# Renewing the sample states in the FFN instead of in the head groups' stage

## The chip, the cores and the metric

One Trainium2 chip; the kernel runs on one of its cores. The metric is the time in microseconds (us) that one execution takes on the device, the median of several runs. The engines are TensorE (PE in the profile; its weight loads are PEld), VectorE (DVE), ScalarE (ACT), GpSimd (POOL) and SyncE (SP), which here only issues loads.

## The reference

One step of a hybrid decoder layer, on 256 tokens of a prompt and on 8 samples of 8 tokens each, in float32. The part that matters here is the state of the SSD heads (a recurrence over tokens). Per sample b there are 32 heads with a state of 64 x 128 each. In the reference it is, in short:

```python
states = einsum("bcsgn,bcsgr,bcsgrp->bcgrpn", bc, decay_states, xdt)   # B^T (decay * dt * x)
final  = chunk_decay * init_state + states                             # the state after the 8 tokens
y_off  = einsum("bctgn,bcgrpn,bctgr->bctgrp", cc, states_in, exp(da_cs))   # C times the old state
...
y = y_diag + y_off + d_skip * x
```

For the samples the old state is an input (`state_ssm`, 8 x 32 x 64 x 128, 8.4 MB) and the new one an output of the same size. Two things are done with an old state: C times it goes into y, and so into everything that follows; and it is renewed, that is, scaled by the decay over the eight tokens, and grown by a product of B and of x times its step and decay. The renewed state is only an output: nothing in the layer reads it.

After the heads come an output projection, a norm, and an FFN: a projection up to 11264 columns, a convolution over three tokens, a gate, and a projection down.

## The kernel before

All 320 tokens (256 + 64) are the moving operand of every weight matmul. Each weight matrix is read once, in slabs of 128 x 1024 numbers (`slab`, L110 to L124): SP loads a slab into one of three buffers, ACT rounds it to `whi` (L117), DVE subtracts to make `wlo` (L119), and TensorE multiplies three times per block of 128 x 128 (`accumulate`, L126 to L130: whi by the high part of x, whi by the low part, wlo by the high part), 24 matmuls per slab. `project` (L152) makes 512 columns of a projection up, and `chunk_out` (L199) the share that 512 rows have in a projection down.

The stages in order: the input projection with the gated MLP (gate), which `chunk_out` adds to the output; then, from L686, the head groups' stage, four groups of eight heads (`ssd(g)`, L713), with the projections of z and of the next group's x between them; the last chunks of the output projection; a norm (L993 to L1034); the FFN (L1038 on), in eleven groups of 512 columns: `ffn_up(g+1)` and then `chunk_out(ffn_w_down, g)`; the last norm.

Side work is written as generators that stand in the list `bg`. `tick` (L140) moves the first of them on by one step; `project` and `chunk_out` call it after their slabs, `rate` times (1 or 2). `finish` runs a task to its end. This fixes the order in which instructions are traced. A planner then orders each engine's queue by priority and by its own cost model: slabs have a high priority, evacuations of PSUM under `first()` a higher one, side work none. On the chip each queue runs in that order; an instruction that waits holds all behind it on its engine, and an SP load that waits for a buffer holds the loads behind it.

The states, four pairs i per group, each of two tiles `st` of 128 x 512 (samples i and 4 + i):

- `load_state(i)` (L719) loads a pair on SP, into five buffers. Two pairs are loaded when the group begins, the others when a pair has been worked off (L846).
- `with_c(i, st)` (L793, matmuls L798, out `yo_ps`) multiplies by C: eight small matmuls, traced a step after a yield.
- `picked(i)` (L801) makes `bm` on ACT: B's rows of this pair of samples, out of `bsp` by the column mask `bsel`.
- `shrunk(i, st)` (L806) scales both tiles on POOL by `tote` (exp of the sum of the decays, made in `steps`, L498).
- `grown(st, bm)` (L811) multiplies `bm` by `xsp` into a bank `up_ps` (L814), and DVE adds it to the tile (L815).
- `store_state` (L818) writes the tile out, issued from ACT's queue.
- `xsp` is `xq` split into a high and a low part: a copy on ACT (L778) and a subtraction of the upper 64 rows on DVE (L779).

Groups 0 to 2 do all of it in `ssd`. Group 3 only applies C there; its states are loaded a second time and renewed by `renewals` (L822) while the last two chunks of the output projection run (L979, L985), and its last pair of matmuls stands behind the last chunk (L995), ahead of the sums of the norm.

PSUM has eight banks: four for weight matmuls (tag "mm"), four (tag "ms", `misc`) for everything else, `yo_ps` and `up_ps` among them.

Of the kernel before, what the change touches and what calls it, by code (L numbers as in the profile page):

```python
# [9 lines left out]
F32 = mybir.dt.float32  # L10
# [7 lines left out]
P = 128  # L18
# [16 lines left out]
def hybrid_step(  # L35
# [267 lines left out]
    dacs_d = dr.tile([NH, NT + NS], F32, name="dacs_d")  # L303
    tot_d = dr.tile([NH, NB], F32, name="tot_d")


# [45 lines left out]
    def by_token(ps, x, c):  # L352

        pe.transpose(ps, x[:, P * c:P * c + P], ident)

    def fourfold(out, x):
# [5 lines left out]
    with ExitStack() as mctx:  # L362
# [43 lines left out]
        ed = op.tile([P, 4, 4], F32, name="ed")  # L406
        tote = op.tile([P, NH, NB], F32, name="tote")

        def steps():
# [276 lines left out]
        with tc.tile_pool(name="sd", bufs=1) as sd:  # L686
# [8 lines left out]
            for c in range(4):  # L695
# [11 lines left out]
            def by_head(ap):  # L707
                return ap.rearrange("p (h d) -> p h d", d=64)

# [3 lines left out]
            def ssd(g):  # L713
# [18 lines left out]

                sts = [load_state(i) for i in range(2)]

# [41 lines left out]
                x0d = decayed(0, 0)  # L776
                xsp = sd.tile([P, 2, 512], F32R, tag="xsp", name="xsp", bufs=1)
                act.copy(xsp, xq)  # L778
                dve.tensor_tensor(out=xsp[64:], in0=xq[64:], in1=xsp[64:].bitcast(F32), op=ALU.subtract)  # L779
# [20 lines left out]

                def picked(i):  # L801
                    bm = sd.tile([P, 2, P], F32R, tag="bm", name="bm", bufs=2)
                    act.activation(bm, bsp[:, :, bs].bitcast(F32), AF.Copy, scale=bsel[:, i:i + 1])
                    return bm

                def shrunk(i, st):  # L806
                    for h in range(2):
                        pool.tensor_tensor(out=by_head(st[h]), in0=by_head(st[h]),  # L808
                                           in1=tote[:, h0:h0 + 8, 4 * h + i:4 * h + i + 1].to_broadcast([P, 8, 64]), op=ALU.mult)

                def grown(st, bm):  # L811
                    for h in range(2):
                        ps = misc("up_ps")
                        made = pe.matmul(ps, bm[:, h], xsp[:, h], start=True, stop=True)  # L814
                        dve.tensor_tensor(out=st[h], in0=st[h], in1=ps, op=ALU.add)  # L815
                    return made.ins

                def store_state(i, st, by=act):  # L818
                    for h in range(2):
                        by.dma_start(o_ssm_s[4 * h + i, g], st[h])  # L820

                def renewals():  # L822
                    sts = [load_state(i) for i in range(2)]
                    yield
                    for i in range(4):
                        st, bm = sts.pop(0), picked(i)
                        shrunk(i, st)
                        yield
                        made = grown(st, bm)
                        store_state(i, st, act if i < 3 else pool)  # L830
                        if i < 2:
                            sts.append(load_state(2 + i))
                        yield made

                for i in range(4):
# [5 lines left out]
                    yield  # L841
                    if g < 3:
                        shrunk(i, st)
                        grown(st, bm)
                        store_state(i, st)
                    if i < 2:  # L846
                        sts.append(load_state(2 + i))

# [144 lines left out]
            with first():  # L993
                with tc.issue_after(pd_last[-1]):
                    made = next(rest[0])  # L995
                with tc.issue_after(made):
                    most = token_sums(sq2)
                with tc.issue_after(sums_ins[-1]):
                    ps = token_sums(*one)
                with tc.issue_after(sums_ins[-1]):  # L1000
                    made = next(rest[1])
                r = rsqrt_by_root(most, ps, 1.0 / D)
                behind = rsqrt_ins[-1]
                with tc.issue_after(behind):
                    next(rest[1])
                with tc.issue_after(made):
                    r2b = spread(r)
# [30 lines left out]
    with tc.tile_pool(name="fp", bufs=1) as fp:  # L1038
# [226 lines left out]
```

## Time and profile before

| | us |
|---|---|
| median of three runs | 1821.66 |
| lowest and highest | 1821.31, 1822.76 |
| the profiled execution's span | 1821.3 |
| the input projection and the gate, about | 0 to 440 |
| the head groups' stage, about | 440 to 760 |
| the last chunks of the output projection, about | 760 to 855 |
| norm and beginning of the FFN, about | 855 to 905 |
| the FFN, about | 905 to 1800 |
| last norm and output | 1800 to 1821 |

The profiled execution's own time is its span, 1821.3 us, which agrees with the fastest of the three runs; nothing beside the span is counted.

How to read the profile: a line such as `L814 PE MATMUL up_ps<-xsp,bm` is line 814 of the kernel, on TensorE, writing the tile `up_ps` from `xsp` and `bm`. A row of waits, `PE yo_ps L798 <- DMA st: 3.1, 3, 1.2`, says that this line waited for that producer for 3.1 us in total, three times, 1.2 at the longest. A matmul's bar is longer than its share of the time, since matmuls overlap: the distance from start to start is what it costs. The granted clock is a share of TensorE's full clock.

### The profile page before, as it was taken

What the parts mean: (1) busy time and instruction counts of PE and PEld (TensorE: products, weight loads), DVE (VectorE), ACT (ScalarE), POOL (GpSimd) and SP (SyncE); (2) the same over time, 40 slices, a digit from 0 to 9 for tenths busy, and PEclk for the clock granted to TensorE, in tenths of its full rate; (3) what the DMA queues carried; (4) which work ended last, traced back from release to release, by engine and by line L of the source; (5) the groups of instructions that cost most, each with busy time, mean ns of one, the idle gap of its engine ahead of it and who ended that gap; (6) DMA issues with size and microseconds to landing.
All of it is one profiled execution on the core that took longest, in us unless ns stands there. A gap on an engine that the chain in (4) does not pass through costs nothing.

```text
span 1821.3 us, 31186 instructions
## 1 busy us (share of the span) xinstructions
PE 1789.4 (98%) x12222; PEld 1751.6 (96%) x12222; DVE 1182.3 (65%) x2029; ACT 798.1 (44%) x1102; POOL 304.5 (17%) x626
## 2 busy tenths in 40 slices
PE   8999999999999999999899999999999999999998
PEld 8999999999889899999899999999999999999997
DVE  5449664557977868677776465647465665756575
ACT  6444454334535445444455433333334343433334
POOL 3102200000331312104521010101111010101004
PEclk9999999999999999999999999999999999999999
DMA  8656544455566565556454545444545445454542
GB/s 268 186 150 189 159 132 152 155 157 176 189 192 189 162 196 173 156 159 206 148 149 151 150 153 153 151 152 151 153 152 154 150 154 150 151 148 153 151 154 99
DMA packets 222947, 294.66 MB, mean 162 GB/s; under 512 B 16752, under 2 KB 150736, under 8 KB 222608
## 3 DMA queue, kind: packets, MB, share of 16 engines
q1 hardware_dynamic: 210544, 270.21, 48.6%
q10 hardware_dynamic: 9872, 14.82, 2.2%
q0 software_dynamic: 2384, 7.64, 1.4%
q8 instruction: 96, 1.57, 0.4%
q14 instruction: 51, 0.42, 0.1%
HBM read 277.80 MB, written 14.82 MB: 161 GB/s over the span
## 4 chain that ended last, share of the span: by engine, by line
PE 88%; DVE 4%; DMA 2%; issue 2%; POOL 2%; ACT 1%; ACTq 0%; POOLq 0%; DVEq 0%
PE ps L128 18%; PE ps L130 18%; PE ps L129 18%; PE pd L128 9%; PE pd L130 9%; PE pd L129 9%; DVE wlo L119 1%; PE y_ps L888 1%; DMA cT<-in_x_tok 1%; POOL acc_mix L1023 1%; ACT whi L117 1%; DMA cs<-dacs_d 1%; DMA st<-in_state_ssm 0%; POOL st L808 0%; PE sg L650 0%
## 5 line engine op out<-in xcount | busy, mean ns | idle before, releaser
L119 DVE TENSOR_TENSOR wlo<-wraw,whi 128x1024 fp32r<-128x1024 f32 (+1 forms) x476 | 592.0, 1244 | 455.4 <-ACT whi L117 452.8
L117 ACT CAST whi<-wraw 128x1024 fp32r<-128x1024 f32 (+1 forms) x476 | 496.3, 1043 | 730.2 <-PE ps L129 443.7
L128 PE MATMUL ps<-h_hi,whi 128*128 128x320 f32 x2528 | 787.5, 312 | 8.6 <-ACT whi L117 5.6
L130 PE MATMUL ps<-h_hi,wlo 128*128 128x320 f32 x2528 | 783.9, 310 | 4.3 <-DVE wlo L119 4.3
L129 PE MATMUL ps<-h_lo,whi 128*128 128x320 f32 x2528 | 782.8, 310 | 0.0
L128 PEld LDWEIGHTS ps<-h_hi,whi 128*128 128x128 f32 x2528 | 477.5, 189 | 14.2 <-ACT whi L117 6.9
L130 PEld LDWEIGHTS ps<-h_hi,wlo 128*128 128x128 f32 x2528 | 477.2, 189 | 6.6 <-DVE wlo L119 6.4
L129 PEld LDWEIGHTS ps<-h_lo,whi 128*128 128x128 f32 x2528 | 477.5, 189 | 0.7 <-issue 0.5
L128 PE MATMUL pd<-fhi,whi 128*128 128x320 f32 x704 | 217.0, 308 | 0.0
L129 PE MATMUL pd<-flo,whi 128*128 128x320 f32 x704 | 217.0, 308 | 0.0
L130 PE MATMUL pd<-fhi,wlo 128*128 128x320 f32 x704 | 217.0, 308 | 0.0
L128 PE MATMUL pd<-ohi,whi 128*128 128x320 f32 x448 | 140.8, 314 | 0.0
L129 PE MATMUL pd<-olo,whi 128*128 128x320 f32 x448 | 139.5, 311 | 0.0
L130 PE MATMUL pd<-ohi,wlo 128*128 128x320 f32 x448 | 139.4, 311 | 0.0
L128 PEld LDWEIGHTS pd<-fhi,whi 128*128 128x128 f32 x704 | 132.1, 188 | 0.0
L129 PEld LDWEIGHTS pd<-flo,whi 128*128 128x128 f32 x704 | 132.1, 188 | 0.0
L130 PEld LDWEIGHTS pd<-fhi,wlo 128*128 128x128 f32 x704 | 132.1, 188 | 0.0
L1074 POOL COPY ptf<-pad 128x2 f32<-128x2 f32 x88 | 20.5, 233 | 618.1 <-DVE pad L1062 617.4
L211 DVE TENSOR_TENSOR acc_ffn<-acc_ffn,pd 128x320 f32<-128x320 f32 x160 | 77.5, 484 | 38.7 <-PE pd L130 37.4
L128 PEld LDWEIGHTS pd<-ohi,whi 128*128 128x128 f32 x448 | 84.8, 189 | 2.9 <-issue 1.6
L130 PEld LDWEIGHTS pd<-ohi,wlo 128*128 128x128 f32 x448 | 84.7, 189 | 1.0 <-issue 1.0
L129 PEld LDWEIGHTS pd<-olo,whi 128*128 128x128 f32 x448 | 84.8, 189 | 0.5 <-issue 0.2
(297 smaller groups left out, 1599.4 us busy)
## 6 DMA issues: line engine op xcount, KB each, us to landing
wraw<-in_ffn_w_up SPq DMA_DIRECT2D x176, 512.0 KB, 3.7
wraw<-in_w_in SPq DMA_DIRECT2D x144, 512.0 KB, 3.7
wraw<-in_ffn_w_down SPq DMA_DIRECT2D x88, 512.0 KB, 3.5
wraw<-in_w_out SPq DMA_DIRECT2D x64, 512.0 KB, 3.5
st<-in_state_ssm SPq DMA_DIRECT2D x40, 256.0 KB, 3.8
out_ssm_state_sample<-st ACTq DMA_DIRECT2D x30, 256.0 KB, 3.6
cs<-dacs_d SPq DMA_DIRECT2D x16, 320.0 KB, 4.3
xr<-in_xT SPq DMA_DIRECT2D x4, 640.0 KB, 4.8
```

What stands on the lines that cost most here:

```text
L117: act.copy(hi[:, :m], raw[:, :m])
L119: dve.tensor_tensor(out=lo[:, :m], in0=raw[:, :m], in1=hi[:, :m].bitcast(F32), op=ALU.subtract)
L128: pe.matmul(ps, whi, xhi, start=first, stop=False)
L129: pe.matmul(ps, whi, xlo, start=False, stop=False)
L130: return pe.matmul(ps, wlo, xhi, start=False, stop=last).ins
L211: dve.tensor_tensor(out=acc[:, nb, :], in0=acc[:, nb, :], in1=ps[:, :NT], op=ALU.add)
L888: pe.matmul(ps[64 * i:64 * i + 64, cols], w(hl), x(hl, m, cpx), tile_position=(0, 64 * i), **flags)
L1023: added.append((dve if kt < 2 else pool).tensor_tensor(out=a, in0=a, in1=xr[q][:, k, :], op=ALU.add).ins)
L1074: pool.tensor_copy(ptf[:, k, :], pad[:, 256:258])
```

## The change

In the head groups' stage only C is applied to the states, for all four groups. All sixteen pairs are loaded a second time in the FFN and renewed there, by a task in `bg` that begins with `ffn_up(1)` and is finished at the latest ahead of the last chunk. Its operands are kept in DRAM until then: `xq` of each group (512 KB each), `bsp` (512 KB) and `tote` (128 KB) are stored from ACT's queue, and loaded again from SP's. The split of `xq` into `xsp` moves to the FFN too, in two halves. In the head groups' stage the state tiles get eight buffers, so that a group's four pairs are there together. In the FFN they get four, and the operands lie in two tiles that the output projection no longer needs.

```diff
+    xq_d = dr.tile([4, P, 2, 512], F32, name="xq_d")
+    bsp_d = dr.tile([P, 2, 512], F32, name="bsp_d")
+    tote_d = dr.tile([P, NH, NB], F32, name="tote_d")
...
+            tote = op.tile([P, NH, NB], F32, name="tote")
             sp.dma_start(tote, tot_d.unsqueeze(0).broadcast_to([P, NH, NB]))
             act.activation(tote, tote, AF.Exp)
+            yield
+            act.dma_start(tote_d, tote)
...
+            act.dma_start(bsp_d, bsp.bitcast(F32))
...
-                    st = [sd.tile([P, 512], F32, tag="st", name="st", bufs=5) for _ in range(2)]
+                    st = [sd.tile([P, 512], F32, tag="st", name="st", bufs=8) for _ in range(2)]
...
-                sts = [load_state(i) for i in range(2)]
+                sts = [load_state(0), load_state(1)]
...
+                sts.append(load_state(2))
                 yield
+                act.dma_start(xq_d[g], xq)
...
-                xsp = sd.tile([P, 2, 512], F32R, tag="xsp", name="xsp", bufs=1)
-                act.copy(xsp, xq)
-                dve.tensor_tensor(out=xsp[64:], in0=xq[64:], in1=xsp[64:].bitcast(F32), op=ALU.subtract)
...
+                sts.append(load_state(3))
                 yield
...
-                def picked(i):
...
-                def shrunk(i, st):
...
-                def grown(st, bm):
...
-                def store_state(i, st, by=act):
...
-                def renewals():
...
-                for i in range(4):
-                    if g < 3:
-                        bm = picked(i)
+                for i in range(4):
                     yield
-                    st = sts.pop(0)
-                    with_c(i, st)
+                    with_c(i, sts[i])
                     yield
-                    if g < 3:
-                        shrunk(i, st)
-                        grown(st, bm)
-                        store_state(i, st)
-                    if i < 2:
-                        sts.append(load_state(2 + i))
...
-                    rest.extend([renewals(), final()])
-                    next(rest[0])
+                    rest.append(final())
...
-            bg.append(chain(repeat(None, 1), islice(rest[0], 4)))
             chunk_out(w_out, 6, *res[2], False, rate=2)
...
-            bg.append(islice(rest[0], 3))
...
                 with tc.issue_after(pd_last[-1]):
-                    made = next(rest[0])
-                with tc.issue_after(made):
                     most = token_sums(sq2)
...
+        def renewals():
+
+            kept = hp.tile([P, 4, NT], F32R, tag="ohi", name="kept").rearrange("p k n -> p (k n)")
+            more = hp.tile([P, 4, NT], F32R, tag="olo", name="xsp").rearrange("p k n -> p (k n)")
+            tote = kept[:, :NH * NB].bitcast(F32).rearrange("p (h b) -> p h b", b=NB)
+            bsp = kept[:, 256:512].rearrange("p (h n) -> p h n", h=2)
+            bms = [kept[:, 512 + 256 * i:768 + 256 * i].rearrange("p (h n) -> p h n", h=2) for i in range(2)]
+            xsp = more[:, :1024].rearrange("p (h n) -> p h n", h=2)
+            sp.dma_start(tote, tote_d)
+
+            def load(g, i):
+
+                st = [fp.tile([P, 512], F32, tag="st", name="st", bufs=4) for _ in range(2)]
+                for h in range(2):
+                    sp.dma_start(st[h], state_ssm[4 * h + i, g])
+                return st
+
+            ahead = [load(0, 0)]
+            yield
+            for g in range(4):
+                h0 = 8 * g
+                sp.dma_start(bsp.bitcast(F32), bsp_d[:, :, P * g:P * g + P])
+                for h in range(2):
+                    raw = fp.tile([P, 512], F32, tag="raw", name="raw", bufs=1)
+                    sp.dma_start(raw, xq_d[g, :, h])
+                    yield
+                    yield
+                    act.copy(xsp[:, h], raw)
+                    dve.tensor_tensor(out=xsp[64:, h], in0=raw[64:], in1=xsp[64:, h].bitcast(F32), op=ALU.subtract)
+                    yield
+                for i in range(4):
+                    st = ahead.pop(0)
+                    bm = bms[i % 2]
+                    act.activation(bm, bsp.bitcast(F32), AF.Copy, scale=bsel[:, i:i + 1])
+                    for h in range(2):
+                        pool.tensor_tensor(out=by_head(st[h]), in0=by_head(st[h]),
+                                           in1=tote[:, h0:h0 + 8, 4 * h + i:4 * h + i + 1].to_broadcast([P, 8, 64]), op=ALU.mult)
+                    yield
+                    yield
+                    if (g, i) != (3, 3):
+                        ahead.append(load(g + (i + 1) // 4, (i + 1) % 4))
+                    for h in range(2):
+                        ps = misc("up_ps")
+                        pe.matmul(ps, bm[:, h], xsp[:, h], start=True, stop=True)
+                        dve.tensor_tensor(out=st[h], in0=st[h], in1=ps, op=ALU.add)
+                        yield
+                    yield
+                    for h in range(2):
+                        act.dma_start(o_ssm_s[4 * h + i, g], st[h])
+                    yield
+
         NG = NF // 4
         nxt = ffn_up(0)
+        grow = renewals()
+        bg.append(grow)
...
             if g == NG - 1:
+                finish(grow)
                 root_table(pd_last[-1])
```

More of the change, by code (lines that the diff above doesn't have):

```diff
@@ L354, in by_token, with by_head @@
         pe.transpose(ps, x[:, P * c:P * c + P], ident)
+    def by_head(ap):
+        return ap.rearrange("p (h d) -> p h d", d=64)
     def fourfold(out, x):
@@ L406, in hybrid_step @@
         ed = op.tile([P, 4, 4], F32, name="ed")
-        tote = op.tile([P, NH, NB], F32, name="tote")
         def steps():
@@ L705, in hybrid_step @@
                         dve.tensor_tensor(out=b[rs], in0=ps[rs], in1=b[rs].bitcast(F32), op=ALU.subtract)
-            def by_head(ap):
-                return ap.rearrange("p (h d) -> p h d", d=64)
+            act.dma_start(bsp_d, bsp.bitcast(F32))
             x_of = {0: x0}
@@ L799, in with_c @@
                                       start=i == 0, stop=i == 3, tile_position=(0, row))
-                def picked(i):
-                    bm = sd.tile([P, 2, P], F32R, tag="bm", name="bm", bufs=2)
-                    act.activation(bm, bsp[:, :, bs].bitcast(F32), AF.Copy, scale=bsel[:, i:i + 1])
-                    return bm
-                def shrunk(i, st):
-                    for h in range(2):
-                        pool.tensor_tensor(out=by_head(st[h]), in0=by_head(st[h]),
-                                           in1=tote[:, h0:h0 + 8, 4 * h + i:4 * h + i + 1].to_broadcast([P, 8, 64]), op=ALU.mult)
-                def grown(st, bm):
[L812 to L816, printed above, removed]
-                def store_state(i, st, by=act):
-                    for h in range(2):
-                        by.dma_start(o_ssm_s[4 * h + i, g], st[h])
-                def renewals():
-                    sts = [load_state(i) for i in range(2)]
-                    yield
-                    for i in range(4):
-                        st, bm = sts.pop(0), picked(i)
-                        shrunk(i, st)
-                        yield
-                        made = grown(st, bm)
-                        store_state(i, st, act if i < 3 else pool)
-                        if i < 2:
-                            sts.append(load_state(2 + i))
-                        yield made
-                for i in range(4):
-                    if g < 3:
-                        bm = picked(i)
-                    yield
-                    st = sts.pop(0)
-                    with_c(i, st)
-                    yield
-                    if g < 3:
-                        shrunk(i, st)
-                        grown(st, bm)
-                        store_state(i, st)
-                    if i < 2:
-                        sts.append(load_state(2 + i))
+                for i in range(4):
+                    yield
+                    with_c(i, sts[i])
+                    yield
                 for r in range(2):
@@ L1000, in hybrid_step @@
                 with tc.issue_after(sums_ins[-1]):
-                    made = next(rest[1])
+                    made = next(rest[0])
                 r = rsqrt_by_root(most, ps, 1.0 / D)
@@ L1004, in hybrid_step @@
                 with tc.issue_after(behind):
-                    next(rest[1])
+                    next(rest[0])
                 with tc.issue_after(made):
```

## The prediction

> **What bounds the kernel now.** I read the page first, then the table of busy time by stage, then TensorE's waits stage by stage, then the timeline around the longest of them.
>
> ```profile
> span 1821.3 us, 31186 instructions
> PE 1789.4 (98%) x12222; PEld 1751.6 (96%) x12222; DVE 1182.3 (65%) x2029; ACT 798.1 (44%) x1102; POOL 304.5 (17%) x626
> ```
>
> TensorE is busy for 98% of the span, so at most 32 us (1821.3 - 1789.4) of plain idle time can be won. The question is where they lie. Columns below: stretch, its length, then for each engine its busy time and instruction count, granted clock, DMA share, GB/s.
>
> ```profile
> 440.00:760.00 320.00, 311.74 (x2222) 285.63 (x2221) 254.20 (x485) 151.77 (x230) 79.61 (x99) 0.99 0.59 184
> 760.00:855.00 95.00, 94.87 (x647) 94.23 (x646) 69.04 (x123) 44.91 (x67) 17.67 (x15) 1.00 0.57 183
> 855.00:905.00 50.00, 41.70 (x256) 39.13 (x255) 42.12 (x64) 26.72 (x46) 27.74 (x34) 0.95 0.43 137
> 950.00:1400.00 450.00, 450.00 (x3071) 450.00 (x3070) 265.28 (x429) 183.72 (x232) 54.87 (x176) 1.00 0.50 152
> 1800.00:1822.00 22.00, 13.04 (x63) 8.84 (x61) 12.32 (x28) 4.96 (x9) 7.86 (x7) 0.83 0.31 120
> ```
>
> In the FFN TensorE has no gap at all: 3071 matmuls in 450 us are 146.5 ns each, so a slab of 24 takes 3.52 us. The head groups' stage (440 to 760) leaves 8.3 us idle, the hand-over to the FFN (855 to 905) 8.3 us, the tail 9.0 us. The change touches the first of these, so its gain is to be found in this stage's waits:
>
> ```profile
> PE yo_ps L798 <- DMA st<-in_state_ssm: 3.1, 3, 1.2
> PE up_ps L814 <- DVE st L815: 2.0, 1, 2.0
> PE tsum L263 <- DVE ssq L282: 1.1, 1, 1.1
> PE up_ps L814 <- DVE xsp L779: 1.1, 1, 1.1
> PE y_ps L888 <- DVE cs L877: 0.8, 1, 0.8
> ```
>
> These add up to 8.1 us, the whole of the idle time there. Three rows, 6.2 us, belong to the states: a state that has not landed (3.1), and renewing matmuls that wait for a bank or an operand (2.0 + 1.1).
>
> **The change part by part.** *The waits.* The two up_ps rows leave this stage with the matmuls that wait: -3.1 us. The yo_ps row should go too. Now five buffers serve a group, and a state is loaded only when an older one has been scaled, grown and stored; afterwards eight buffers hold the whole group, the loads are issued in its first three steps and each buffer is free as soon as C has been applied to it. A load lands in 3.8 us (row further down), and from the issue of the last pair of states to its use lie more than six steps. So -3.1 us. For each the bounds are 0, if another wait takes the place, and its full row; I take the full rows, since the DVE, which would be late next, loses work as well (below).
>
> *The clock.* After the longest wait the matmuls run slowly for a while:
>
> ```profile
> 485.60 0.50 PE L814 MATMUL up_ps<-xsp,bm 128*128 128x512 f32 x1 [1.97 <-DVE st L815]
> ...
> 486.89 0.47 PE L128 MATMUL pd<-ohi,whi 128*128 128x320 f32 x1
> ...
> 490.09 0.34 PE L128 MATMUL pd<-ohi,whi 128*128 128x320 f32 x1
> ```
>
> ```profile
> 487.00:490.30 3.30, 3.30 (x15) 3.30 (x14) 3.30 (x5) 1.31 (x4) 0.61 (x3) 0.52 0.26 80
> ```
>
> From 486.89 to 490.09 twelve matmuls take 3.20 us, 267 ns each, 120 ns over the usual 146.5: 1.5 us lost at a granted clock of 0.52. Bounds 0 and 1.5; I take 1.5, because the slow stretch begins 1.3 us after the end of the 1.97 us wait and nothing else stopped TensorE near it. The Trainium skill ("TensorE: Matmul & The Clock Gate", Part 1: The HAM clock gate) says that the clock falls to half after an idle window of about 3.4 us. By that figure a wait of 1.97 us would not have been enough, there would be no such term, and the forecast would be 1.5 us higher; the row shows the half clock after the shorter wait, so I follow the row.
>
> *The order on TensorE.* A pair of renewing matmuls between the matmuls of the weights costs less than one that follows C's matmuls:
>
> ```profile
> 536.86 0.74 PE L814 MATMUL up_ps<-xsp,bm 128*128 128x512 f32 x2
> 537.43 0.31 PE L128 MATMUL ps<-h_hi,whi 128*128 128x320 f32 x1
> ```
>
> ```profile
> 812.27 0.62 PE L814 MATMUL up_ps<-xsp,bm 128*128 128x512 f32 x2
> 812.73 0.31 PE L128 MATMUL pd<-ohi,whi 128*128 128x320 f32 x1
> ```
>
> By the starts of the next matmuls the pair took 0.57 us behind C and 0.46 us alone. Twelve pairs leave the stage and all of them then stand among weight matmuls: between 0 and 12 x 0.11 = 1.3 us; I take 1.0, since one or two of them stand alone already. Otherwise the pairs' 0.46 us only move: TensorE is full where they go. The three pairs of the last group that are moved from 760 to 855 gain nothing, as that stretch is full as well (94.87 of 95). The last pair is a small loss:
>
> ```profile
> 855.90 0.63 PE L814 MATMUL up_ps<-xsp,bm 128*128 128x512 f32 x2
> 856.37 0.72 PE L263 MATMUL tsum<-ones,sq 128*128 128x1 f32 x6
> 857.42 0.83 PE L263 MATMUL tsum<-ones,sq 128*128 128x1 f32 x6 [0.33 <-ACT sq L297]
> ```
>
> It fills time before sums that wait for ACT's square in any case; its removal saves nothing there, and it costs 0.46 us in the FFN: +0.5 (bounds 0 and 0.5).
>
> *What is added to the FFN.* Durations, min/median/max in ns, from the lines as they run now:
>
> ```profile
> L808 POOL TENSOR_TENSOR st<-st,tote x32: 1057/1065/2378, 459.7 to 831.7; 128x512 f32<-128x512 f32 x32
> L815 DVE TENSOR_TENSOR st<-st,up_ps x32: 671/680/689, 466.2 to 857.1; 128x512 f32<-128x512 f32 x32
> L803 ACT ACTIVATE bm<-bsp,bsel x16: 493/508/511, 450.8 to 817.3; 128x256 fp32r<-128x256 f32 x16
> L778 ACT CAST xsp<-xq x4: 1045/1050/1052, 455.5 to 718.8; 128x1024 fp32r<-128x1024 f32 x4
> L779 DVE TENSOR_TENSOR xsp<-xq,xsp x4: 1222/1223/2049, 458.7 to 721.5; 64x1024 fp32r<-64x1024 f32 x4
> L820 ACTq DMA_DIRECT2D out_ssm_state_sample<-st x30: 338/338/1282, 466.9 to 838.0; - x30
> ```
>
> DVE: 32 x 0.68 + 4 x 1.22 = 26.7 us. ACT: 16 x 0.51 + 4 x 1.05 = 12.3 us, and 32 x 0.34 = 10.9 us of issuing stores. POOL: 32 x 1.07 = 34 us, 76 at the longest duration. The renewals yield 121 times; the FFN ticks after each slab but those of its first and last steps, 24 times per group, so they run for 121 x 3.52 = 426 us, some five of the eleven groups, and are through well before the last chunk. Over that time DVE goes from 59% (265.28 of 450) to about 65%, ACT from 41% to about 46%. SP issues 32 state loads and 13 of operands. Traffic: 8.4 MB of states in and 8.4 out, 2.1 of xq, 0.4 of the rest, 19.3 MB in 426 us, 45 GB/s on top of 152. The head groups run at 184 GB/s with such traffic today:
>
> ```profile
> wraw<-in_w_in SPq DMA_DIRECT2D x45, 512.0 KB, 4.2
> ...
> st<-in_state_ssm SPq DMA_DIRECT2D x37, 256.0 KB, 3.8
> out_ssm_state_sample<-st ACTq DMA_DIRECT2D x24, 256.0 KB, 3.6
> ```
>
> ```profile
> wraw<-in_ffn_w_up SPq DMA_DIRECT2D x176, 512.0 KB, 3.7
> ```
>
> A weight slab lands there in 4.2 us against 3.7 in the FFN, and TensorE waited for no slab. What covers all this is the lead with which slabs are made:
>
> ```profile
> 1201.28 1.05 ACT L117 CAST whi<-wraw 128x1024 fp32r<-128x1024 f32 x1 [2.47 <-PE ps L129]
> ```
>
> ```profile
> 1202.36 1.23 DVE L119 TENSOR_TENSOR wlo<-wraw,whi 128x1024 fp32r<-128x1024 f32 x1 [2.29 <-ACT whi L117]
> ```
>
> ACT starts a slab when TensorE has released one of three buffers, so two slabs, 7.04 us, lie ahead; 2.31 us later (1203.59) the new one is ready: 4.7 us of lead. The densest stretch of the FFN is where the second half is evacuated:
>
> ```profile
> 1233.00:1255.00 22.00, 22.00 (x152) 22.00 (x151) 19.55 (x41) 10.72 (x14) 5.93 (x16) 1.00 0.47 148
> ```
>
> A pair of states takes six steps, 21 us, so such a stretch gets one pair, 1.36 us of DVE, at times half of an xsp (0.6), into 2.45 us of idle time, with the lead behind it. I put the FFN at 0. Bounds: 0, and 16 pairs at one POOL operation each that shows in full, 17 us (the third rival).
>
> *New waits in queues.* SP's state load waits until a buffer has been stored: the store is issued three steps (10.5 us) before and lands in 3.6. SP's load of the second half of xq waits for the DVE that splits the first, one step earlier; behind it stand weight loads, and 4.7 us of lead. On ACT each store waits for the DVE's add, two steps earlier, with the next cast behind it. On TensorE the renewing matmul waits for bm (0.5 us, two steps earlier). All of these I cost at 0 for the same cover. The operands' stores (four of xq, one of B, one of decays) are 6 x 0.34 us on ACT, which has over half its time free.
>
> *What DVE and POOL lose in the head groups' stage.* 24 adds and the four splits, 24 x 0.68 + 4 x 1.22 = 21 us of DVE's 254, and POOL's 24 scalings. That is why I let no new wait in: DVE is the engine that would be late next.
>
> **The sum.** -3.1 - 3.1 - 1.5 - 1.0 + 0.5 = -8.2 us on the profiled 1821.3 gives 1813.1. That execution is the fastest of the three shown; their median, 1821.66, lies 0.36 us above it, so I forecast **1813.5**.
>
> **The rivals.**
> *More goes than the states' own waits (1810.1).* With 21 us less on DVE the sums no longer wait for ssq (1.1) nor y_ps for cs (0.8), and the slow clock after the former (674.5 to 678) shrinks; without it 1813.5 - 1.9 = 1811.6, with its 1.5 us 1810.1. For it: both waits are for DVE. Against: cs also waits for its own load, ssq for a chain through ACT.
>
> ```profile
> 674.50:678.00 3.50, 3.50 (x15) 3.50 (x14) 2.46 (x10) 1.04 (x1) 0.00 (x0) 0.52 0.81 262
> 454.00:486.00 32.00, 30.03 (x206) 27.20 (x205) 30.13 (x60) 17.90 (x28) 13.73 (x23) 1.00 0.51 164
> ```
>
> *DVE keeps the pace (1819.1).* Ahead of the longest wait DVE is busy for 30.13 of 32 us. If its convolutions and sums merely stop TensorE a little later, only the loads' 3.1 us are won, less 0.5 in the FFN: 1821.66 - 2.6. For it: that stretch. Against: some 4 us of its work leave.
>
> *The FFN pays (1830.5).* DVE takes its instructions in order, and the add of a state stands in front of evacuations and splits. If POOL has not finished scaling by then, they all wait:
>
> ```profile
> DVE st L815 <- POOL st L808: 5.1, 5, 3.7
> ```
>
> The add comes two steps (7.0 us) after the scaling was issued, which itself takes 2.1 us a pair, 4.8 at the longest. If in each of 16 pairs 1.06 us shows on TensorE, that is +17.0 on the forecast: 1830.5. It is slower than before from 0.5 us per pair on. Against it: 2.2 to 4.9 us of cover and then the lead. The Trainium skill ("SBUF — State Buffer", Who interferes with whom) speaks for it: a VectorE instruction with two SBUF inputs and a GpSimd one that reads SBUF exclude each other for a whole instruction. The trace agrees: a split took 2.08 us instead of 1.23 beside two scalings. By that rule 32 x 1.06 = 34 us of holding are moved into the FFN.
>
> ```profile
> 486.36 2.08 DVE L119 TENSOR_TENSOR wlo<-wraw,whi 128x1024 fp32r<-128x1024 f32 x1
> ```
>
> **How the numbers follow.** Forecast 0.52, more goes 0.12, DVE keeps the pace 0.22, the FFN pays 0.14. The range 1809.0 to 1821.5 holds the first three and leaves out the last and a little below. What a measurement of this kernel can tell from no change is about 0.2%, 3.6 us: the first two cases are faster (0.64), the third is within it (0.22), the last slower (0.14).
>
> **What would show it.** Right: in the head groups' stage no wait of yo_ps for a state and none of up_ps, 5 to 6 us less idle time, a full clock at 487; in the FFN still no wait. Wrong: TensorE waits for wlo or up_ps between 910 and 1340, a split's lead well under 4 us, DVE's add waiting for POOL, or waits for cs and ssq grown in the head groups.

## The result, and the profile after

The changed kernel takes 1810.26 us (median of four runs, 1808.37 to 1812.42) against 1822.21 us for the kernel before, now also four runs (1821.31 to 1823.06): a ratio of 0.9936, 95% interval 0.9924 to 0.9949, so 11.7 us or 0.64% less. The forecast was 1813.5 us, 8.2 us less; the time lies within the range, and next to the figure of the first rival (1810.1).

A word on the base. The changed kernel's profiled execution took 1812.42 us at a span of 1810.7 us: an execution's time is its span and 1.7 us around it. The profiled execution of before, with its span of 1821.3, must then be the one of 1823.06 us, the slowest of the four and not the fastest, as the prediction had taken it.

The page of the kernel after, and its busy time by stage (the stages' bounds are shifted by what was won):

```profile
span 1810.7 us, 31220 instructions
PE 1784.3 (99%) x12222; PEld 1750.2 (97%) x12222; DVE 1183.4 (65%) x2033; ACT 798.7 (44%) x1106; POOL 303.2 (17%) x624
```

```profile
440.00:755.00 315.00, 314.41 (x2311) 293.19 (x2311) 238.18 (x477) 150.85 (x226) 45.06 (x70) 1.00 0.56 179
755.00:850.00 95.00, 91.72 (x605) 90.07 (x605) 67.71 (x128) 45.35 (x71) 18.95 (x17) 0.96 0.47 154
850.00:900.00 50.00, 45.48 (x287) 44.03 (x286) 37.43 (x47) 22.41 (x36) 30.04 (x31) 0.93 0.58 179
945.00:1340.00 395.00, 395.00 (x2676) 393.62 (x2675) 262.56 (x415) 167.16 (x221) 79.00 (x174) 1.00 0.60 193
1790.00:1811.00 21.00, 12.65 (x61) 8.45 (x59) 11.98 (x27) 4.96 (x9) 7.71 (x6) 0.84 0.33 125
```

In the head groups' stage TensorE idles 0.6 us instead of 8.3, at a full clock. The 3.3 us of idle time between 755 and 850 are no new waits: the hand-over to the FFN now begins there, and its longest wait, 2.1 us for `h_hi`, lay between 855 and 905 before. While the renewals run in the FFN (945 to 1340) it has no gap, though 193 GB/s move instead of 152. TensorE's waits in the head groups' stage, all of them:

```profile
PE tsum L263 <- DVE ssq L282: 0.5, 1, 0.5
```

Of the five rows of before one is left, at half its size. Where the time went is best read from three marks that both kernels have: C's matmuls (`yo_ps`), the first matmuls of the FFN's first step (`ps_one`), and the hand-over at the end (`x1p`). The rows give the first and the last start. Before:

```profile
L798 PE MATMUL yo_ps<-st,cb_cms x128: 379/391/403, 459.0 to 731.0; 128*32 128x256 f32 x128
L128 PE MATMUL ps_one<-h_hi,whi x16: 307/308/313, 914.4 to 922.7; 128*128 128x320 f32 x16
L1147 PE MATMUL x1p<-acc_mix,ident x22: 432/433/863, 1803.8 to 1815.1; 128*128 128x320 f32 x22
```

After:

```profile
L804 PE MATMUL yo_ps<-st,cb_cms x128: 378/391/404, 462.0 to 713.1; 128*32 128x256 f32 x128
L128 PE MATMUL ps_one<-h_hi,whi x16: 304/309/310, 896.6 to 904.9; 128*128 128x320 f32 x16
L1159 PE MATMUL x1p<-acc_mix,ident x22: 432/433/803, 1793.5 to 1804.7; 128*128 128x320 f32 x22
```

| stretch, us | before | after | difference |
|---|---|---|---|
| beginning to the first C matmul | 459.0 | 462.0 | +3.0 |
| first to last C matmul | 272.0 | 251.1 | -20.9 |
| last C matmul to the FFN's first step | 183.4 | 183.5 | +0.1 |
| FFN | 889.4 | 896.9 | +7.5 |
| last norm and output | 17.5 | 17.2 | -0.3 |
| span | 1821.3 | 1810.7 | -10.6 |

So the head groups' stage gave 21 us, much more than forecast (8.7 us by the four terms, and 5.6 us for 24 moved matmuls), and the FFN took 7.5 us back, the price of all 32 matmuls. The adds in the FFN and the scalings ahead of them:

```profile
L1129 DVE TENSOR_TENSOR st<-st,up_ps x32: 676/686/690, 948.0 to 1339.1; 128x512 f32<-128x512 f32 x32
```

```profile
L1120 POOL TENSOR_TENSOR st<-st,kept x32: 1057/1138/2455, 882.4 to 1303.1; 128x512 f32<-128x512 f32 x32
```

The adds spread over 391 us; from the FFN's first step (896.6) to the last add it is 443 us, against the 426 that the prediction counted from the steps. DVE never waited for POOL at an add.

### The profile page after: what moved, and what is told of

Its sections match the earlier page's. It is cut to its first block, busy times and chain, and to the rows that moved or that the text cites. A ratio compares the mean times of both kernels' runs of the same rounds, so it can differ in the third digit from the quotient of the medians.

```text
span 1810.7 us, 31220 instructions
## 1 busy us (share of the span) xinstructions
PE 1784.3 (99%) x12222; PEld 1750.2 (97%) x12222; DVE 1183.4 (65%) x2033; ACT 798.7 (44%) x1106; POOL 303.2 (17%) x624
## 4 chain that ended last, share of the span: by engine, by line
PE 93%; DVE 2%; DMA 2%; ACT 1%; POOL 1%; issue 1%; ACTq 0%; DVEq 0%; POOLq 0%
PE ps L128 19%; PE ps L130 19%; PE ps L129 19%; PE pd L128 10%; PE pd L130 10%; PE pd L129 10%; DMA wraw<-in_w_in 1%; PE y_ps L851 1%; DVE wlo L119 1%; POOL acc_mix L981 1%; PE yo_ps L804 1%; ACT whi L117 0%; PE sg L658 0%; PE up_ps L1128 0%; PE xt_ps L357 0%
## 5 line engine op out<-in xcount | busy, mean ns | idle before, releaser
L211 DVE TENSOR_TENSOR acc_ffn<-acc_ffn,pd 128x320 f32<-128x320 f32 x160 | 77.1, 483 | 35.8 <-PE pd L130 34.8
```

Of the source, the lines that this page charges most:

```text
L211: dve.tensor_tensor(out=acc[:, nb, :], in0=acc[:, nb, :], in1=ps[:, :NT], op=ALU.add)
```

## The experiments

The theory after the result: TensorE's waits in the head groups' stage came from the renewals' POOL and DVE work there and from late states, and the FFN pays for the moved matmuls alone. The rivals are named with each run. "As changed" means the time of the changed kernel, 1809.8 to 1810.3 us; a difference from it is taken from 1809.78.

**Both kernels once more, for second traces.** No edit.

> The kernel before, unchanged, for a second trace. If the first 440 us differ between the two kernels' profiles (3.0 us in the changed kernel's disfavour) only by chance, this trace will show another offset there, by 1 us or more; if the beginning is the same in every execution, it agrees within 0.5 us with the first trace up to 440 us. In the head groups' stage both views expect the same waits again: yo_ps for states near 3 us, up_ps near 3 us, y_ps and tsum near 2 us, and two stretches at half clock.

> The changed kernel, unchanged, for a second trace. Chance at the beginning: its first 440 us come out up to 3 us shorter than in the first trace. A cost of the change at the beginning (the planner's order of the first loads): again 3 us longer than before. From 440 us on: no wait of yo_ps or up_ps, about 20 us less than before up to the end of the output projection, 7.5 us given back in the FFN.

Measured: 1821.98 us (ratio to before 1.0005, 0.9994 to 1.0017) and 1809.78 us (0.9940, 0.9925 to 0.9955). The first C matmul starts at 459.5 us in the second trace of before and at 458.4 in that of after, so the 3.0 us at the beginning were chance. From the first to the last C matmul the second traces show 269.6 and 251.4 us, and for the FFN 889.4 and 897.0. The gain of the stage is 18 to 21 us; the FFN's 7.5 us come out alike in both pairs. In the second trace of before, the same lines wait in the head groups' stage, as expected; the two rows that differ most from the first trace (3.1 and 2.0) are:

```profile
PE yo_ps L798 <- DMA st<-in_state_ssm: 4.2, 5, 1.3
PE up_ps L814 <- DVE st L815: 1.3, 1, 1.3
```

The two stretches at half clock, expected too, are not there. The stretch with the long wait for DVE and that of the norm's sums, in the first and in the second trace:

```profile
478.00:495.00 17.00, 15.03 (x92) 12.30 (x85) 15.12 (x23) 7.94 (x16) 8.48 (x13) 0.90 0.55 173
665.00:682.00 17.00, 15.88 (x100) 15.62 (x99) 10.62 (x24) 9.83 (x14) 0.00 (x0) 0.90 0.42 125
```

```profile
478.00:495.00 17.00, 15.53 (x104) 12.26 (x103) 15.89 (x24) 8.08 (x16) 9.54 (x14) 1.00 0.55 184
665.00:682.00 17.00, 16.13 (x112) 15.87 (x111) 10.39 (x23) 10.05 (x15) 0.00 (x0) 1.00 0.44 134
```

The granted clock is 0.90 in both stretches of one execution and 1.00 in the other. The waits in them were 2.0 and 1.1 us in the first, 1.3 and 0.9 us in the second; and a wait of 1.2 us for a state in the first execution was followed by no loss of clock. So the length of a single wait does not settle it, and what does is open.

**No renewal.** The task in the FFN is not started; the sample states are neither renewed nor written.

```diff
-        bg.append(grow)
...
-                finish(grow)
```

> The changed kernel without the task in the FFN: the samples' states are not renewed nor written. If the FFN pays for the 32 matmuls alone (32 x 0.235 = 7.5 us), this kernel is 7.5 us faster than the changed one, about 1802.8 us. If the scaling, the adds and the loads cost something too, it is more than 9 us faster. If the FFN hides all, it is within 2 us.

Measured: 1801.82 us (0.9898, 0.9878 to 0.9917), 8.0 us less than the changed kernel.

```profile
L128 PE MATMUL ps_one<-h_hi,whi x16: 307/308/312, 892.6 to 900.9; 128*128 128x320 f32 x16
L1157 PE MATMUL x1p<-acc_mix,ident x22: 432/432/537, 1782.0 to 1793.0; 128*128 128x320 f32 x22
```

The FFN takes 889.4 us, as before the change: the renewals cost 7.5 us in it, 32 x 0.235. Scaling, adds, splits, loads and stores cost nothing there.

**No matmul.** DVE adds the state to itself; the rest of the renewals stays.

```diff
-                        ps = misc("up_ps")
-                        pe.matmul(ps, bm[:, h], xsp[:, h], start=True, stop=True)
-                        dve.tensor_tensor(out=st[h], in0=st[h], in1=ps, op=ALU.add)
+                        dve.tensor_tensor(out=st[h], in0=st[h], in1=st[h], op=ALU.add)
```

> The changed kernel whose renewals leave out the matmul: DVE adds the state to itself, everything else (loads, scaling, masks, splits, stores) stays; the states come out wrong by that term. If TensorE's own 7.5 us are the whole price in the FFN, this is equal to the kernel without renewals, about 7.5 us faster than the changed one. If DVE, POOL or the loads cost time, it lies between the two.

Measured: 1834.82 us (1.0077, 1.0060 to 1.0094), 25 us **slower** than the changed kernel with less work. Neither expectation had that. The adds, and TensorE's longest waits from 900 to 1400:

```profile
L1127 DVE TENSOR_TENSOR st<-st x32: 677/684/1551, 883.8 to 1008.4; 128x512 f32<-128x512 f32 x32
```

```profile
PE tsum L263 <- DVE rs_v L243: 4.3, 1, 4.3
PE ps L130 <- DVE wlo L119: 3.9, 1, 3.9
PE ps_one L130 <- DVE wlo L119: 3.0, 1, 3.0
```

```profile
880.00:1010.00 130.00, 105.25 (x640) 101.25 (x639) 100.59 (x157) 53.17 (x78) 69.60 (x95) 0.89 0.78 254
```

All 32 adds ran within 125 us instead of 391, at the beginning of the FFN: traffic of 254 GB/s, and TensorE busy for 105 of 130 us, with clock lost as well. Here the adds do wait for POOL, and all that stands behind them in DVE's queue waits too:

```profile
DVE st L1127 <- POOL st L1120: 17.8, 9, 3.9
```

This is the mechanism of the prediction's third rival. The reading: the ticks only order the tracing, and the matmul was the one instruction that held a pair back until TensorE came to its place; without it the planner put the rest as early as buffers allowed, into a stretch where TensorE waits for its operands even without them.

**A short matmul**, to test that reading: 64 of the 512 columns, added eight times over by DVE.

```diff
-                        pe.matmul(ps, bm[:, h], xsp[:, h], start=True, stop=True)
-                        dve.tensor_tensor(out=st[h], in0=st[h], in1=ps, op=ALU.add)
+                        pe.matmul(ps[:, :64], bm[:, h], xsp[:, h, :64], start=True, stop=True)
+                        dve.tensor_tensor(out=by_head(st[h]), in0=by_head(st[h]),
+                                          in1=ps[:, :64].unsqueeze(1).to_broadcast([P, 8, 64]), op=ALU.add)
```

> The changed kernel whose renewing matmul takes 64 of its 512 columns; DVE adds these eight times over, so its add stays as long, and still waits for TensorE; the states come out wrong by that. Theory A (in the kernel without the matmul the renewals lost the one thing that ties them to TensorE's progress, ran together at the beginning of the FFN and paid there): here the adds stay spread over some 390 us as in the changed kernel, the FFN has no waits, and the kernel is 4 to 6 us faster than the changed one. Rival B (an add of two operands in SBUF beside POOL is what cost time there): here the add reads PSUM again, so it is also fast, but the adds' spread is then no matter and they may stand anywhere. The two are told apart by the starts of the adds in the trace. Rival C (adds and scalings cost time in the FFN in any case): slower than the changed kernel.

Measured: 1805.39 us (0.9915, 0.9899 to 0.9932), 4.4 us less than the changed kernel's 1809.78. The adds are back in their places, and from 905 us to the end of the FFN TensorE waits for nothing:

```profile
L1129 DVE TENSOR_TENSOR st<-st,up_ps x32: 673/686/690, 945.8 to 1333.1; 128x512 f32<-128x512 f32 x32
```

So theory A's signs came, all three. The time alone does not rule out rival B, since with the matmul the add reads PSUM again as well; but in the kernel without the matmul an add took 857 ns on average, 5 us more for all 32 than as changed, which is too little for 25. How much of the 25 us is DVE's waiting and how much the denser traffic, no run separates. A matmul of 512 columns is what is paid, and its place is what paces the renewals.

**POOL's and DVE's load put back.** In the head groups' stage, after C, groups 0 to 2 scale and add again; the results are thrown away. Then each half of it alone.

```diff
                     with_c(i, sts[i])
                     yield
+                    if g < 3:
+                        for h in range(2):
+                            pool.tensor_tensor(out=by_head(sts[i][h]), in0=by_head(sts[i][h]),
+                                               in1=dec[:, 2, h0:h0 + 8].unsqueeze(2).to_broadcast([P, 8, 64]), op=ALU.mult)
+                        for h in range(2):
+                            dve.tensor_tensor(out=sts[i][h], in0=sts[i][h], in1=sts[i][h], op=ALU.add)
```

> The changed kernel with the old load of POOL and DVE put back into the head groups' stage: after C is applied, groups 0 to 2 scale each state tile on POOL and add it to itself on DVE (24 of each; the results are thrown away). No matmul, no store comes back. Theory A (the waits of sums for ssq and of y_ps for cs went because DVE lost 21 us of work): they return, with a stretch at half clock, and the kernel is 2 to 5 us slower than the changed one. Rival B (these waits hung on the states' matmuls and buffers): no wait returns, the time stays within 1.5 us of the changed kernel.

> Of the load that cost 8 us when POOL's scaling and DVE's add were both put back into the head groups' stage, only the 24 adds on DVE (results thrown away). Theory A (it is DVE's time, 16 us, that makes the waits): at least 5 us slower than the changed kernel. Rival B (it is the chain: DVE's add stands in its queue waiting for POOL's scaling, and what follows it waits too): within 2 us of the changed kernel, and so is POOL's part alone.

> The changed kernel with only the 24 scalings on POOL put back into the head groups' stage (results thrown away). Theory A (DVE's time): within 2 us of the changed kernel. Rival B (the chain from POOL to DVE): within 2 us here and with DVE's part alone, since neither alone makes the chain. Rival C (POOL's reads hold DVE's instructions, or delay POOL's own products for y): 4 us or more slower here.

Measured: both 1818.14 us (0.9989, 0.9980 to 0.9998), DVE alone 1811.50 (0.9950, 0.9934 to 0.9967), POOL alone 1809.45 (0.9941, 0.9921 to 0.9960). Together they cost 8.4 us, apart 1.7 and nothing. The stage from 440 to 755 with both, with DVE's part, with POOL's:

```profile
440.00:755.00 315.00, 309.52 (x2249) 287.24 (x2248) 261.36 (x489) 147.43 (x220) 79.53 (x94) 0.99 0.57 175
```

```profile
440.00:755.00 315.00, 313.65 (x2296) 291.65 (x2294) 250.91 (x499) 150.84 (x225) 44.90 (x70) 1.00 0.56 178
```

```profile
440.00:755.00 315.00, 314.40 (x2303) 292.82 (x2302) 247.00 (x481) 149.94 (x225) 77.47 (x94) 1.00 0.55 178
```

POOL's scalings alone raise DVE's busy time from 238 to 247 us, with no DVE instruction added. The add itself, with POOL beside it and without:

```profile
L816 DVE TENSOR_TENSOR st<-st 128x512 f32<-128x512 f32 x24 | 24.7, 1055 | 0.0
```

```profile
L813 DVE TENSOR_TENSOR st<-st 128x512 f32<-128x512 f32 x24 | 16.2, 686 | 9.2 <-PE yo_ps L804 9.1
```

That is 1055 ns a piece on average against 686. With both, DVE is busy almost without a gap from 484 to 499 us, and the instruction that takes C's result (`xdt`) comes late in its queue:

```profile
PE y_ps L857 <- DVE xdt L820: 3.9, 1, 3.9
```

The wait is followed by a stretch at half clock:

```profile
498.40:503.00 4.60, 4.46 (x28) 3.90 (x29) 3.11 (x8) 1.52 (x2) 0.00 (x0) 0.50 0.69 229
```

With DVE alone, y_ps waits for cs as long as before the change:

```profile
PE y_ps L854 <- DVE cs L843: 0.8, 1, 0.8
```

The 8.4 us are more than the 2 to 5 expected. Of the later two expectations rival B had both times right, but not the mechanism: no add waits for POOL's scaling (0.0 us in its row). It is DVE's load with POOL's on top, which lengthens DVE's instructions.

The 8.4 us are not what this load cost in the kernel before. There the adds read one operand from PSUM and were not lengthened (15.9 us for 24, against 24.7 here), DVE also had the four splits, and no y_ps waited for xdt. Between the first and the last C matmul DVE was busy for 219.86 us before and for 193.24 after: 26.6 us less, where the prediction counted 21 of DVE's own instructions. The other 5 to 6 us are instructions that stayed and were longer beside POOL's scalings: a split took 1318 ns on average there before and 1263 after.

**Late loads, five buffers.** The states are loaded as before, the third and fourth pair after the first and second have been multiplied by C.

```diff
-                    st = [sd.tile([P, 512], F32, tag="st", name="st", bufs=8) for _ in range(2)]
+                    st = [sd.tile([P, 512], F32, tag="st", name="st", bufs=5) for _ in range(2)]
...
-                sts.append(load_state(2))
...
-                sts.append(load_state(3))
...
+                    if i < 2:
+                        sts.append(load_state(2 + i))
```

> The changed kernel with five state buffers in the head groups' stage and the third and fourth pair loaded only when the first and second have been multiplied by C, as before. Theory A (the early loads into eight buffers removed the yo_ps wait of 3.1 us): yo_ps waits for loads again, 2 to 4 us, and the kernel is that much slower than the changed one. Rival B (the buffers come free at once when C is all that uses them, whatever their number): no such wait, within 1 us of the changed kernel.

Measured: 1809.32 us (0.9940, 0.9925 to 0.9954), as changed, and no wait of yo_ps:

```profile
PE tsum L263 <- DVE ssq L282: 0.9, 1, 0.9
```

The eight buffers did nothing. Why the states came late before is seen on SP, whose loads wait for a buffer, here before and in this run:

```profile
SPq L723 <- DMA out_ssm_state_sample<-st: 28.3, 18, 4.7
```

```profile
SPq L729 <- PE yo_ps L802: 33.8, 13, 6.2
```

Before, a load waited most for the store of the pair that had the buffer, which comes after scaling and adding; now it waits most for C's matmuls, and no matmul of C waits for a state.

**The matmuls put back** into the head groups' stage, beside those of the FFN: 24 of the same size, unread.

```diff
+                            ps = misc("up_ps")
+                            pe.matmul(ps, bsp[:, h, bs], bsp[:, h], start=True, stop=True)
```

> The changed kernel with 24 matmuls of the renewals' size (operands that lie there, results unread) put back behind C's matmuls in the head groups' stage; those of the FFN stay. Theory A (a pair beside C's small matmuls costs more than its 0.47 us, because weight loads are laid open on both sides: 1.3 us in the up_ps rows and 2.7 us in the yo_ps rows of the accounts): 7.5 to 10 us slower than the changed kernel. Rival B (C's matmuls were slower only because their states landed in two parts): 5.5 to 6.5 us slower, 24 x 0.235 = 5.6.

Measured: 1814.58 us (0.9963, 0.9950 to 0.9976), 4.8 us more than as changed, a little below what either theory expected.

```profile
L804 PE MATMUL yo_ps<-st,cb_cms x128: 378/391/404, 458.6 to 715.6; 128*32 128x256 f32 x128
```

In the trace it is 257.0 us from first to last against 251.4: 5.6 us, 24 x 0.235, as rival B has it. Standing beside C's matmuls costs a pair nothing extra.

**POOL four times over** in the FFN.

```diff
-                    for h in range(2):
+                    for h in (0, 0, 0, 0, 1, 1, 1, 1):
                         pool.tensor_tensor(out=by_head(st[h]), in0=by_head(st[h]),
```

> The changed kernel with each scaling in the FFN done four times over: 96 more POOL operations of 1.06 us or more; the states come out wrong. Theory A (two steps and the lead of 4.7 us cover POOL): a pair's scaling takes 8.5 us or more instead of 2.1, beyond the two steps of 7.0 us, so the add begins to wait for POOL, by 1.5 to 5 us a pair, but most of that lies within the lead; 0 to 5 us slower than the changed kernel. Rival B (POOL's hold on DVE shows on TensorE as soon as it grows): 16 pairs at 1 us or more each, over 15 us slower. Rival C (POOL does not matter at all): no wait of the add for POOL, the same time.

Measured: 1821.34 us (1.0005, 0.9995 to 1.0016), 11.6 us more than as changed, between A and B; the whole gain is gone. The trace is that of the slowest of ten executions, 1826.81 us, so its losses are larger than the median's. With four times the scalings, the stretch of the renewals and the splits in it:

```profile
940.00:1350.00 410.00, 404.44 (x2726) 400.82 (x2725) 300.41 (x427) 171.40 (x229) 201.79 (x272) 1.00 0.60 187
```

```profile
L119 DVE TENSOR_TENSOR wlo<-wraw,whi 128x1024 fp32r<-128x1024 f32 x112 | 156.9, 1403 | 73.6 <-ACT whi L117 73.0
```

As changed, DVE is busy for 271.7 us of this stretch and a split takes 1258 ns. No add waits for POOL, so theory A's mechanism did not come. DVE's instructions grow longer beside POOL's, and TensorE then waits for DVE: in the renewals' stretch mostly for banks that DVE has not emptied yet (L211), and in the FFN's first step, which takes 15 us instead of 8 by its first matmuls:

```profile
PE pd L128 <- DVE acc_ffn L211: 3.9, 4, 1.8
```

```profile
L128 PE MATMUL ps_one<-h_hi,whi x16: 307/309/468, 896.5 to 911.4; 128*128 128x320 f32 x16
```

**Denser renewals**, three steps a pair instead of six.

```diff
                     yield
-                    yield
                     if (g, i) != (3, 3):
...
                         dve.tensor_tensor(out=st[h], in0=st[h], in1=ps, op=ALU.add)
-                        yield
-                    yield
```

> The changed kernel with the renewals' steps closer together: three steps a pair instead of six (one between scaling and matmul, none ahead of the store). Theory A (the matmul in TensorE's order paces everything, and one step of 3.5 us still covers POOL's 2.1 us): the adds end near 1130 us instead of 1335, waits of a few us in the FFN at most, within 3 us of the changed kernel. Rival B (the spread over 390 us is what keeps the FFN free of waits): over 6 us slower, with waits for wlo or up_ps as in the kernel without the matmul.

Measured: 1810.13 us (0.9943, 0.9925 to 0.9961), as changed.

```profile
L1128 DVE TENSOR_TENSOR st<-st,up_ps x32: 675/680/689, 942.5 to 1122.5; 128x512 f32<-128x512 f32 x32
```

The adds end at 1122 us, and from 905 us on the FFN still has no wait. What matters is that they are tied to TensorE, not how far they are spread. In all kernels without waits they also begin after the FFN's first step; no run moved their beginning alone. No run points to a kernel that does the whole computation faster than the changed one.

## Why the prediction was right, and where it was not

**The side and the mechanism were right.** The gain lies in the head groups' stage, where states and DVE made TensorE late, and the FFN hides everything but the matmuls. The signs named for it came: no wait of yo_ps for a state and none of up_ps, a full clock at 487 us, no wait in the FFN; the idle time fell by 7.7 us instead of 5 to 6.

**The waits.** Forecast -6.2 us; all three rows went, as forecast. The two others that were left in place (ssq 1.1, cs 0.8) went to 0.5 in sum as well. The reason given for yo_ps, eight buffers and early loads, fell: five serve as well once C alone uses them.

**The first mis-sized step is "So -3.1 us" for the yo_ps row.** A row of waits counts only from the end of the last matmul's bar. In the kernel before, one pair whose second tile landed late looks like this:

```profile
536.29 0.64 PE L798 MATMUL yo_ps<-st,cb_cms 128*32 128x256 f32 x8
...
541.04 0.62 PE L798 MATMUL yo_ps<-st,cb_cms 128*32 128x256 f32 x2
542.72 0.63 PE L798 MATMUL yo_ps<-st,cb_cms 128*32 128x256 f32 x6 [1.06 <-DMA st<-in_state_ssm]
543.28 0.72 PE L814 MATMUL up_ps<-xsp,bm 128*128 128x512 f32 x2
```

Eight matmuls took 0.57 us where the whole pair was there (536.29 to 536.86, the next start), and 2.24 us here: 1.67 us more, of which the row counts 1.06. Added up from start to start over both traces of before, and compared with after, late states cost 5.2 us where the rows say 3.1, and 6.4 us where they say 4.2.

**The second is "What DVE and POOL lose", costed at nothing beyond the waits named.** The waits for cs and ssq went with that load; by starts they were 2.0 us in the first pair of traces and 1.6 in the second. That they hung on it is shown for cs: its wait comes back with DVE's adds alone, at 1.7 us for the kernel. The prediction counted 21 us of DVE's own instructions and left out the 5 to 6 us by which POOL's scalings lengthened others. The rival "more goes than the states' own waits", given 0.12, had these two waits and met the time to 0.2 us. That is in part luck: its sum has 3.0 us for the clock, which one execution of two lost, and 1.0 us for the order on TensorE, which none did, and it lacks what the late states cost beyond their row.

**The clock.** -1.5 us was right for one place of one execution. That execution had two such places, and the second trace of before has none, so the term is 0 to about 3 us by execution. The forecast followed the row. The idle window of about 3.4 us that the Trainium skill states ("TensorE: Matmul & The Clock Gate", Part 1: The HAM clock gate) fits the second trace, in which waits of 1.3 us and less left the clock alone, and not the first. One trace was not enough to decide.

**The order on TensorE.** -1.0 us was wrong: matmuls put back beside C cost 0.235 each and no more.

**The sum, by traces.** Between the first and the last C matmul 20.9 us went in the first pair of traces and 18.2 in the second. By starts these are 5.6 and 5.6 for the moved matmuls (forecast as cancelling, and they do), 5.2 and 6.4 for late states, 3.5 and 3.0 for the waits of up_ps, 2.0 and 1.6 for cs and ssq, and 2.7 and 0 for the clock. Some 2 us in each are not assigned. So the forecast's 8.2 us against 11.7 measured were short by the late states and by cs and ssq, and long by the order; how the clock weighs in the medians is not known. The filler's +0.5 us is lost in the scatter of the stretch behind the last C matmul (183.2 to 184.8 us in four traces), and so are the 1.4 us of the six matmuls moved out of it; the clock differs there by execution too, 0.83 against 0.71 from 860 to 870 us in the two traces of before.

**The FFN.** 0 beyond the moved matmuls was right to 0.1 us. The rival "the FFN pays" names a real mechanism that this kernel stays clear of. Without the matmul, adds wait for POOL as it was written. With four times the scaling no add waits, but DVE's instructions grow longer, and that costs 11.6 us, 0.7 a pair; the actual load is covered.

**The base.** The forecast took the profiled execution for the fastest; taken from the median of before, 1822.21, -8.2 us would have given 1814.0.

## What to carry to other kernels

Here TensorE was full where the work went, and what it paid there was the moved matmuls, 0.235 us each; all else was free as long as the other engines' lead covered it. To price a late operand, go from start to start of the matmuls around it: the wait row showed 3.1 us of 5.2. Before counting an engine's relief by its own instructions, count what another engine's traffic does to their lengths: put back, the two loads cost 8 us together and under 2 apart. Side work that a planner may place freely needs something that ties it to the bottleneck: the matmul did it here, and leaving it out made the kernel 25 us slower.

## What the runs showed of the hardware

An add of two SBUF operands took 1055 ns on average beside POOL's scalings and 686 without them; the Trainium skill ("SBUF — State Buffer", Who interferes with whom) states this exclusion, and the rows agree. The renewing add, with one operand in PSUM, was not lengthened: 676 to 690 ns as changed and 672 to 691 with four times the scalings. The half clock after waits of 1 to 2 us is not a fixed property of a kernel: the mean granted clock was 0.90 against 1.00 over the same 17 us in two executions. The time of an execution was 1.7 us more than its span.
